# Weight sums of an encoder layer: accumulating transfers in place of VectorE additions

## The chip, the cores and the metric

The kernel runs on one core of a Trainium2 chip. The metric is the device time of one execution in microseconds. Before the change it is 1713.99 us, the median of three runs (1713.55 to 1715.02).

## The reference, cut to what matters

One layer of a bidirectional encoder, for two groups of 256 tokens with 1024 channels each, all in float32:

```
x = x + 0.5 * swiglu(rms_norm(x, g1), w_gate1, w_up1, w_down1)      # width 2816
u = rms_norm(x, gm);  proj = u @ w_in                               # one combined projection
o_na  = neighborhood_attention(q, k, v, rpb)                        # 16 heads of 64
o_ssd = two-way scan of conv(x, B, C), gated and group-normed
o_mem = memory_attention(q_mem, k_mem, v_mem)                       # 256 memory tokens
x = x + (sum_b sigmoid(gate_b) * (o_b @ w_br_b)) @ w_out
x = x + 0.5 * swiglu(rms_norm(x, g2), w_gate2, w_up2, w_down2)
```

Most of the work is products of 512 token rows with weight matrices.

## The kernel before, in words

**Products.** Every float32 matrix is split into a high part, rounded to a shorter format that TensorE takes, and a low part, the rest. A product is then three matmuls: high by high, low by high, high by low. For the weights the split is made on the fly: ScalarE casts the raw block `wr` to `wh` (line 349) and VectorE subtracts, `wl = wr - wh` (through the helper at line 248). The matmuls of a block product are at line 627 (`product`), those of plain products at lines 605 to 607 (`unit`).

**Seven products instead of eight.** The large projections (gate and up of both FFNs; query of the memory branch, values, and both halves of query and key of the neighbourhood branch) use a two-by-two block scheme with seven block products per column block. `seven` builds them: for each product p it adds an item to the list `ITEMS` with the blocks to load, the block to use, and `sums`, pairs of blocks (d, x) of which x is added into d before d is used. Products 5, 6, 7 and 4 have one sum each: B11 += B12, B11 += B22, B12 += B22, B11 += B21. So d is a raw block in SBUF of 128 x 1024 float32, often already used by an earlier product, and x is another one. A column block 512 wide is cut into two halves along the contraction (h = 0, 1), so it has 14 items and eight sums; the last block of an FFN is 256 wide and has seven items and four sums.

**Stages.** `make_plan` lists the items: the first FFN (column blocks 0 to 5; its block 0 is made without the scheme, so it has no sums), the memory keys and values, then a middle stage with four sets of seven products (`qm`, `v`, `qk` 0, `qk` 1, kind `sv`), then gates, branches, convolutions and scan, the output projection, and the second FFN (blocks 0 to 5). In an FFN, down-projection items of the block before stand between the pairs of products. In the sets nothing stands between them in the plan, but small tasks (attention and the like) are stepped in.

**Loading and summing.** Raw blocks live in a ring of nine slots (`RING`); `fetch` loads them ahead by SyncE's queue (line 302). A slot becomes free when the last use of its block is done, which is a split or a sum. `ahead` splits items up to two ahead of the product in hand; three pairs of `wh` and `wl` exist, so the cast of an item waits for the product three items before. `sums` makes the additions of the next items. If an item's flag `dma` is false, VectorE adds (line 248 again, output `wr`). If it is true, GpSimd's queue issues a transfer from SBUF to SBUF that adds to its destination (line 323), and `ahead` calls for it right after the split two items before:

```
if it.dma:
    self.G.dma_start(out=d, in_=v, accum_op=ALU.add)
else:
    self.tt(d, d, v, ALU.add)
```

Before the change the flag is true for three column blocks: set `qk` 1 and blocks 0 and 1 of the second FFN.

**Order.** The program is written in the order of `PLAN`. The framework keeps track of which instruction needs which, and orders each engine's queue when it builds the kernel; the trace shows sums on VectorE well ahead of where the program calls for them. Within a queue, the chip runs in order.

Of the kernel before, what the change touches and what calls it, by code (L numbers as in the profile page):

```python
# [39 lines left out]
ITEMS = []  # L40


def add_item(*args, **kw):
    ITEMS.append(Item(*args, **kw))
    return len(ITEMS) - 1
# [7 lines left out]
def seven(kind, p, key, block, nh):  # L53

    out = []
    for h in range(nh):  # L60
        n = lambda b: f"{kind}{key}.{h}.{b}"
        blk = lambda b: block(int(b[1]) - 1, int(b[2]) - 1, h)
        loads, src, sums = {1: (["B11"], "B11", []), 2: (["B21"], "B21", []), 5: (["B12"], "B11", [("B11", "B12")]),
                            6: (["B22"], "B11", [("B11", "B22")]), 3: ([], "B22", []), 7: ([], "B12", [("B12", "B22")]),
                            4: (["B21."], "B11", [("B11", "B21.")])}[p]
        _, _, nk, _, m = blk("B11")
        it = add_item(n(src), nk, m, [(n(b), blk(b)) for b in loads], [tuple(n(b) for b in t) for t in sums])
        ITEMS[it].dma = bool(sums) and (kind == "sv" and key == ("qk", 1) or kind == "gu" and key in (("ffn2", 0), ("ffn2", 1)))
        out.append((kind, (*key, p, h, nh), [it]))
    return out  # L70


def make_plan():
# [10 lines left out]
    def ffn(f):  # L84
# [5 lines left out]
        for ci, (c0, w) in enumerate(CBLOCKS + ((DFF, 0),)):  # L90
            n, down = w // 256, list(range(4)) if before else []

            def next_down():
                if down:
                    mp = down.pop(0)
                    s.append(("d", (f, ci - 1, mp), [plain(f + "_w_down", before[0], before[1], 256 * mp, 256)]))

            def part(p, ci=ci, c0=c0, w=w, n=n):
                s.extend(seven("gu", p, (f, ci), lambda i, j, h: (f + ("_w_up", "_w_gate")[j], 4 * i + 4 // n * h, 4 // n, c0, w), n))

            if f == "ffn1" and ci == 0:
                for j, mat in enumerate(("_w_up", "_w_gate")):
                    for c in range(4):
                        n = 1 if j == c == 0 else 2
                        s.append(("pl", (f, j, c), [plain(f + mat, 2 * c + i, n, c0, w) for i in range(0, 2, n)]))
            else:
                for p in PRODUCTS if w else ():
                    if p == 4 and ci == 0:
                        rest = part
                        continue  # L110
                    part(p)
                    if p == 1 and ci == 1 and f == "ffn2":
                        rest(4)
                    if p in ((5, 6, 3, 7) if n == 2 else (5, 3, 7, 4)):
                        next_down()
            for _ in range(4):
                next_down()
            before = (c0 // 128, w // 128)
# [15 lines left out]
    def sv(i, p):  # L134
        kind, c, *cols = sets[i]
        s.extend(seven("sv", p, (kind, c), lambda i, j, h: ("w_in", 4 * i + 2 * h, 2, cols[j], 512), 2))
# [1387 lines left out]
```

## Time and profile before

| what | value |
|---|---|
| median of three runs | 1713.99 us |
| profiled execution | 1712.59 us |
| span of its trace, first to last instruction | 1710.8 us |
| TensorE matmul (PE) | 1698.3 us busy, 99% |
| VectorE (DVE) | 1248.8 us, 73% |
| ScalarE (ACT) | 906.4 us, 53% |
| GpSimd (POOL) | 21.8 us, 1% |
| bytes moved by DMA | 241.69 MB, mean 141 GB/s |
| granted TensorE clock | 1.000 of full speed |

Busy shares are means over stages with different limits. A matmul is recorded as longer than the distance to the next one, since matmuls are pipelined; so the distance between starts tells the pace. Stretches are given in us from the span's start.

### The profile page before, as it was taken

How to read it: one execution, taken by the hardware profiler on the slowest of the kernel's cores; microseconds unless marked ns; L12 is line 12 of the kernel's file. 1: busy time of each engine (PE TensorE's matmuls, PEld its weight loads, DVE VectorE, ACT ScalarE, POOL GpSimd, SP SyncE). 2: the span in 40 equal slices, each digit the busy share in tenths (PEclk: the TensorE clock that was granted, in tenths of full speed). 3: DMA queues.
4: the chain of work that ended last, by engine and by line, in shares of the span. 5: the costliest groups of instructions: out<-in, count | busy, mean ns of one | idle time of the engine just before them, and what ended most of it. 6: DMA issues, size and time to landing. Idle time of an engine off the chain costs nothing.

```text
span 1710.8 us, 22582 instructions
## 1 busy us (share of the span) xinstructions
PE 1698.3 (99%) x8418; PEld 1396.5 (82%) x8418; DVE 1248.8 (73%) x2003; ACT 906.4 (53%) x1612; POOL 21.8 (1%) x30
## 2 busy tenths in 40 slices
PE   9999999999999999999999999999999999999998
PEld 7888888988888887788887887887788888888887
DVE  7776776877596675746978889888754775776775
ACT  7443443535455566654765677667532564443442
POOL 0000000000000000000000000000000010000000
PEclk9999999999999999999999999999999999999999
DMA  7234234443345675444364545346753487344331
GB/s 268 72 133 148 99 105 141 148 160 97 107 135 188 176 213 186 148 129 166 120 133 132 127 140 139 120 147 164 165 190 107 106 222 202 87 135 146 99 100 50
DMA packets 95070, 241.69 MB, mean 141 GB/s; under 512 B 13680, under 2 KB 24432, under 8 KB 94960
## 3 DMA queue, kind: packets, MB, share of 16 engines
q1 hardware_dynamic: 91504, 227.66, 42.6%
q0 software_dynamic: 3456, 12.58, 4.0%
q8 instruction: 66, 1.08, 0.3%
q14 instruction: 44, 0.36, 0.1%
HBM read 210.70 MB, written 16.92 MB: 133 GB/s over the span
## 4 chain that ended last, share of the span: by engine, by line
PE 54%; DVE 1%; DMA 1%; ACT 0%; issue 0%; SPq 0%; ACTq 0%
PE ac L627 12%; PE m L605 9%; PE m L607 9%; PE m L606 9%; PE m L1174 5%; PE d L606 2%; PE d L607 2%; PE d L605 2%; PE y L1395 2%; PE CB L1345 1%; DMA rw<-scr_n 1%; PE hT L756 1%; PE xT L1334 0%; PE sum L566 0%; DMA rw<-scr_r 0%; PE no L1091 0%
## 5 line engine op out<-in xcount | busy, mean ns | idle before, releaser
L349 ACT CAST wh<-wr 128x1024 fp32r<-128x1024 f32 (+1 forms) x381 | 395.9, 1039 | 594.2 <-PE ac L627 209.3
L248 DVE TENSOR_TENSOR wl<-wr,wh 128x1024 fp32r<-128x1024 f32 (+1 forms) x381 | 460.2, 1208 | 199.9 <-ACT wh L349 187.3
L627 PE MATMUL ac<-wh,sh 128*128 128x512 f32 (+1 forms) x744 | 281.2, 378 | 0.1
L627 PE MATMUL ac<-wh,sl 128*128 128x512 f32 (+1 forms) x744 | 278.1, 374 | 0.0
L627 PE MATMUL ac<-wl,sh 128*128 128x512 f32 (+1 forms) x744 | 278.1, 374 | 0.0
L605 PE MATMUL m<-uh,wh 128*128 128x512 f32 x576 | 229.5, 398 | 0.0
L606 PE MATMUL m<-ul,wh 128*128 128x512 f32 x576 | 224.8, 390 | 0.0
L607 PE MATMUL m<-uh,wl 128*128 128x512 f32 x576 | 224.8, 390 | 0.0
L627 PEld LDWEIGHTS ac<-wh,sh 128*128 128x128 f32 x744 | 140.2, 188 | 24.6 <-ACT wh L349 0.5
L627 PEld LDWEIGHTS ac<-wh,sl 128*128 128x128 f32 x744 | 140.1, 188 | 24.7
L627 PEld LDWEIGHTS ac<-wl,sh 128*128 128x128 f32 x744 | 140.3, 189 | 23.8
L606 PE MATMUL d<-hl,wh 128*128 128x512 f32 x352 | 137.3, 390 | 0.7 <-DVE hl L248 0.7
L605 PE MATMUL d<-hh,wh 128*128 128x512 f32 x352 | 137.4, 390 | 0.5 <-ACT hh L270 0.5
L607 PE MATMUL d<-hh,wl 128*128 128x512 f32 x352 | 137.0, 389 | 0.0
L605 PEld LDWEIGHTS m<-uh,wh 128*128 128x128 f32 x576 | 108.2, 188 | 27.8 <-ACT ct L263 4.2
L607 PEld LDWEIGHTS m<-uh,wl 128*128 128x128 f32 x576 | 108.1, 188 | 23.1 <-issue 0.4
L606 PEld LDWEIGHTS m<-ul,wh 128*128 128x128 f32 x576 | 108.3, 188 | 21.4 <-issue 0.2
L259 DVE SCALAR_TENSOR_TENSOR x<-d,x 128x512 f32<-128x512 f32 x96 | 66.1, 690 | 77.3 <-PE d L607 76.8
L248 DVE TENSOR_TENSOR wr<-wr,wr 128x1024 f32<-128x1024 f32 x88 | 107.4, 1221 | 9.6 <-DMA wr<-in_w 8.4
L263 ACT ACTIVATE e<-rw,lots 128x256 f32<-128x256 f32 (+1 forms) x256 | 97.4, 445 | 2.3 <-DMA rw<-scr_r 2.3
L259 DVE SCALAR_TENSOR_TENSOR cv<-m,params,cv 128x508 f32<-128x508 f32 (+1 forms) x128 | 95.0, 742 | 1.3
L606 PEld LDWEIGHTS d<-hl,wh 128*128 128x128 f32 x352 | 66.1, 188 | 14.8 <-DVE hl L248 1.4
(247 smaller groups left out, 2658.6 us busy)
## 6 DMA issues: line engine op xcount, KB each, us to landing
wr<-in_w SPq DMA_DIRECT2D x315, 512.0 KB
rw<-scr_r SPq DMA_DIRECT2D x64, 256.0 KB
wr<-wr POOLq DMA_DIRECT2D x24, 512.0 KB, 5.8
nv<-scr_v SPq DMA_DIRECT2D x64, 64.0 KB
scr_o<-cv SPq DMA_DIRECT2D x16, 256.0 KB
or<-scr_o SPq DMA_DIRECT2D x16, 256.0 KB
wr<-in_w SPq DMA_DIRECT2D x11, 256.0 KB
x<-in_xT SPq DMA_DIRECT2D x8, 256.0 KB
```

What stands on the lines that cost most here:

```text
L248: self.V.tensor_tensor(out=out, in0=a, in1=b, op=op)
L259: self.V.scalar_tensor_tensor(out=out, in0=a, scalar=s, in1=b, op0=op0, op1=op1)
L263: self.S.activation(out=out, in_=x, func=f, **kw)
L349: self.S.copy(hi[:, :n], t[:, :n])
L605: self.T.matmul(ps[:m], wh[:, kk, :], xh, start=i == 0, stop=False)
L606: self.T.matmul(ps[:m], wh[:, kk, :], xl, start=False, stop=False)
L607: self.T.matmul(ps[:m], wl[:, kk, :], xh, start=False, stop=i == n - 1)
L627: go = lambda l, r, **f: self.T.matmul(ps, l, r, skip_group_check=True, **f)
L756: self.T.transpose(ps[:, (2 * r + t) * 128:(2 * r + t + 1) * 128], o["sg", r, t][:, c * 128:(c + 1) * 128], self.ident)
L1174: go = lambda l, r, **f: self.T.matmul(ps, l, r, skip_group_check=True, **f)
L1345: T.matmul(ps[:, st * 256:(st + 1) * 256], bm[:, b * 256 + st * 128:b * 256 + (st + 1) * 128], cm[:, b * 256:(b + 1) * 256], start=True, s ...
L1395: T.matmul(yb[64 * hp:64 * hp + 64, b * 256:(b + 1) * 256], xt[i][:, (2 * b + st) * 128 + 64 * hp:(2 * b + st) * 128 + 64 * hp + 64], w[hp ...
```

## The change

The condition for the flag `dma` is replaced. All column blocks with sums now have them made by transfers on GpSimd's queue, except block 1 of the first FFN.

```diff
@@ seven @@
         it = add_item(n(src), nk, m, [(n(b), blk(b)) for b in loads], [tuple(n(b) for b in t) for t in sums])
-        ITEMS[it].dma = bool(sums) and (kind == "sv" and key == ("qk", 1) or kind == "gu" and key in (("ffn2", 0), ("ffn2", 1)))
+        ITEMS[it].dma = bool(sums) and key != ("ffn1", 1)
```

Of 112 sums, 24 were transfers and 88 additions on VectorE; now 104 are transfers and 8 are additions. The order of the items, the loads and the splits in the program stays as it is, but for the place where `ahead` calls `sums`.

## Rows read from the trace of the kernel before

**Rows 1.** Page, part 1: busy us (share of the span) x instructions.
```profile
PE 1698.3 (99%) x8418; PEld 1396.5 (82%) x8418; DVE 1248.8 (73%) x2003; ACT 906.4 (53%) x1612; POOL 21.8 (1%) x30
```

**Rows 2.** Waits of TensorE, longest first: us in total, times, longest us.
```profile
PE y L1395 <- DVE e L248: 2.4, 2, 1.5
```

**Rows 3.** Chain of waits, second FFN's blocks 1 and 2: start us, us, what.
```profile
1426.66 5.44 PE ac L627 x24
...
1459.30 6.81 PE ac L627 x30
...
1488.48 5.44 PE ac L627 x24
...
1521.12 6.80 PE ac L627 x30
```

**Rows 4.** Page, part 5: groups of instructions: busy us, mean ns of one, idle before, releasers.
```profile
L248 DVE TENSOR_TENSOR wr<-wr,wr 128x1024 f32<-128x1024 f32 x88 | 107.4, 1221 | 9.6 <-DMA wr<-in_w 8.4
```

**Rows 5.** Groups on TensorE, 445 to 600 us, then 1462 to 1524.
```profile
L627 PE MATMUL ac<-wh,sh 128*128 128x512 f32 x96 | 38.5, 403 | 0.1
...
L627 PE MATMUL ac<-wh,uh 128*128 128x512 f32 x76 | 30.7, 404 | 0.0
...
L605 PE MATMUL d<-hh,wh 128*128 128x512 f32 x32 | 12.4, 389 | 0.0
```

**Rows 6.** Line 323 and its queue: ns min/median/max; share of 16 engines.
```profile
q0 software_dynamic: 3456, 12.58, 4.0%
...
L323 POOL DMA_DIRECT2D wr<-wr x24: 859/869/1118, 583.6 to 1435.8; - x24
...
DMA to landing us min/median/max: 4.5/5.8/8.3
```

**Rows 7.** Timeline, second FFN's block 0: start us, us, instruction, idle before and releaser.
```profile
1371.89 1.22 DVE L248 TENSOR_TENSOR wl<-wr,wh 128x1024 fp32r<-128x1024 f32 x1
...
1373.51 0.87 POOL L323 DMA_DIRECT2D wr<-wr  x1 [3.91 <-DVE y L290]
...
1378.69 1.05 ACT L349 CAST wh<-wr 128x1024 fp32r<-128x1024 f32 x1 [3.85 <-PE ac L627]
...
1381.19 0.39 PE L627 MATMUL ac<-wh,sh 128*128 128x512 f32 x1
...
1381.22 1.05 ACT L349 CAST wh<-wr 128x1024 fp32r<-128x1024 f32 x1 [1.48 <-DMA wr<-wr]
...
1383.91 0.39 PE L627 MATMUL ac<-wh,sh 128*128 128x512 f32 x1
```

**Rows 8.** Stretches: length, busy us of PE, PEld, DVE, ACT, POOL; clock; DMA share; GB/s.
```profile
445.00:504.00 59.00, 58.94 (x265) 47.83 (x265) 52.18 (x70) 32.01 (x51) 0.00 (x0) 1.00 0.38 125
504.00:558.00 54.00, 53.96 (x254) 44.64 (x253) 40.41 (x68) 30.37 (x65) 0.00 (x0) 1.00 0.47 159
...
1352.00:1400.00 48.00, 48.00 (x217) 39.78 (x216) 38.25 (x65) 31.29 (x43) 7.81 (x9) 1.00 0.75 172
1400.00:1462.00 62.00, 62.00 (x283) 51.54 (x282) 37.00 (x42) 26.59 (x32) 6.09 (x7) 1.00 0.75 211
1462.00:1524.00 62.00, 62.00 (x283) 51.35 (x282) 45.21 (x49) 26.80 (x33) 0.00 (x0) 1.00 0.38 119
```

**Rows 9.** Timeline, first FFN's 256-wide block.
```profile
296.01 1.22 DVE L248 TENSOR_TENSOR wl<-wr,wh 128x1024 fp32r<-128x1024 f32 x1 [0.21 <-ACT wh L349]
...
316.38 0.28 PE L627 MATMUL ac<-wh,sh 128*128 128x256 f32 x1
```

**Rows 10.** Timeline, first set of the middle stage.
```profile
461.38 1.23 DVE L248 TENSOR_TENSOR wl<-wr,wh 128x1024 fp32r<-128x1024 f32 x1 [1.50 <-ACT wh L349]
...
471.54 0.39 PE L627 MATMUL ac<-wh,sh 128*128 128x512 f32 x1
```

**Rows 11.** Waits of SyncE's queue: us in total, times, longest us.
```profile
SPq L302 <- DVE wl L248: 998.4, 233, 15.9
...
SPq L302 <- DMA wr<-wr: 33.4, 6, 11.7
```

## The prediction

> **What bounds the kernel now.** I read the busy shares first, then who made TensorE wait and the chain of waits, then the rows of the additions that move, then stretches that already have the new form. The busy shares put PE at 1698.3 of 1710.8 us [rows 1]; all its idle time is 12.5 us. VectorE is busy for 73%. The list of what TensorE waited for, longest first, begins with a VectorE result of the scan, not of the block products: 2.4 us in all, in two instances [rows 2]; all the rest is shorter. The chain of waits then follows TensorE through the product blocks [rows 3]. So TensorE is the bound from its first matmul to its last, and something is worth time only if it removes or adds a TensorE stall. "Busy" can hide a short stall, so beside busy shares I use mean durations and start times of matmuls.
>
> **What is removed.** The row of the additions has 88 instructions, 107.4 us, 1.22 us each [rows 4]. 24 others already go by POOL. The new condition is false for one block of the first FFN only, whose two halves have four sums each: 8 stay, 80 go. That is 80 x 1.221 = 97.7 us of VectorE work, or 1248.8 - 97.7 = 1151 us, 67% of the span. VectorE is off the path, so this is worth at most the stalls that VectorE causes. In the weight products of the middle stage the first of the three matmuls on a weight slice lasts 403 ns (96 of them) and 404 ns (76), where a matmul of the same shape in an FFN block lasts 389 ns [rows 5]: 96 x 14 + 76 x 15 ns = 2.5 us of stall, from whatever cause. That is the ceiling of the gain there; in the large blocks, below, it is 0. I take 0, because the nearest rows with the change in them show no gain.
>
> **What is added.** 80 transfers on POOL's queue. One issue takes 0.87 us of POOL, and from issue to landing 4.5 / 5.8 / 8.3 us pass (least, median, most of 24) [rows 6]. POOL has nothing else after its first microsecond, so queueing there touches only the sums. A sum now ends about 0.4 us (POOL's start behind the releasing split: 1371.89 + 1.22 = 1373.11 to 1373.51 [rows 7]) plus L = 5.8 us after its release instead of 1.2 us. Behind it stand the ACT cast (1.05 us) and the VectorE subtraction (1.22 us) of the same block [rows 7], 2.3 us together, and then the product. ACT is in order: while a cast waits for a transfer, the copies behind it that empty PSUM wait too. SP also is in order: a load that needs the slot of a summed-in block waits for the transfer, not for VectorE.
>
> All of this assumes that the builder, which orders every queue at build time, keeps the order of today's around the sums; where it moves a cast earlier, that cast waits longer.
>
> What hides it, by kind of stretch:
>
> *Six 512-wide FFN blocks, 48 of the 80 sums.* The trace holds this change already. Of two neighbouring blocks of the second FFN, 1400 to 1462 us has its sums on POOL and 1462 to 1524 us has them on VectorE: VectorE busy falls from 45.21 to 37.00 us, DMA share rises from 0.38 to 0.75, and TensorE is 62.00 of 62.00 in both [rows 8]. In the chain of waits the same two pieces start 1459.30 - 1426.66 = 32.64 us apart in the first and 1521.12 - 1488.48 = 32.64 us apart in the second [rows 3]. Cost 0.0 us per block, gain 0.0 us. The other blocks have the same plan, so 6 x 0 = 0. The transfers hide here because a 5.4 us down-projection stands between the pairs of products; without it the cover is that of the next kind.
>
> *Two 256-wide blocks (8 sums).* No block of this shape has transfers yet, so I add up. In the first, the split that releases sum 5 ends at 296.01 + 1.22 = 297.2. With L: sum landed at 297.6 + L, split done at 299.9 + L. This split releases the sum of product 6: landed at 300.3 + 2L, split at 302.6 + 2L. Product 6 starts at 316.38 [rows 9]. Its slack is 13.8 - 2L: zero at L = 6.9 us, +2.2 at the median, -2.8 at 8.3. The block in the second FFN has the same plan. Cost between 0 and 2 x 2.8 = 5.7 us; I take 0, by the median.
>
> *Three sets of the middle stage (24 sums).* The densest is the first, where products follow each other every 2.7 us with nothing between. The split that releases the sum of product 6 ends at 461.38 + 1.23 = 462.6, and its product starts at 471.54 [rows 10]; 462.6 + 0.4 + L + 2.3 = 465.3 + L, so it decides at L = 6.2. Nearest row: the first block of the second FFN is as dense, and its sums are transfers. There the split ends at 1373.1, POOL issues at 1373.51, ACT casts at 1378.69, and the product starts at 1381.19; the next cast waits for its transfer until 1381.22 and its product follows at 1383.91, 2.72 us after, exactly on the pace [rows 7]. 8.1 us from split to product was enough there, and the first set has 8.9. In the other two sets attention work stands between the products and widens the distance. Cost between 0 and 2.1 us (L = 8.3); I take 0.
>
> **DMA engines.** The 24 transfers made 4.0% of 16 engines' span [rows 6]: 0.040 x 1710.8 / 24 = 2.85 us of all sixteen each. In 504 to 558 us a third of the middle stage's sums, eight, would add 22.8 us to a share of 0.47 of 54 us [rows 8]: 0.89. The stretch measured with transfers stood at 0.75 and lost nothing [rows 8]. Below 1 I cost this at 0. SP already spends 998 us waiting for slots behind VectorE's splits and 33 us behind such transfers [rows 11]: its loads run ahead, and five more microseconds on the two slots per block that a sum sets free come out of that lead.
>
> **The sum.** -0 (VectorE) + 0 (large blocks) + 0 (256-wide) + 0 (middle stage) = 0 on the profiled execution: 1712.59 us with a span of 1710.8. The median of the three runs, 1713.99, stands 1.40 us above that execution, so I forecast 1714.0 for the median.
>
> **Rivals.**
>
> *Late landing (slower).* The transfers land later than the median once 104 of them share the engines with the loads. Place: the first set of the middle stage and the two 256-wide blocks. It decides from L = 6.2 there and 6.9 here; at L = 7.85 it costs 1.6 + 2 x 1.9 = 5.4 us: 1719.4. At the worst measured L, 8.3, 2.1 + 5.7 = 7.8: 1721.8. For it: the median is only 0.4 us below the first limit, the worst row is above both, and one cast already waited 1.48 us for a transfer [rows 7]. Against: those transfers landed 5.2 us after issue, in a stretch with a DMA share twice that of a plain FFN block, and both are short places.
> VectorE could also hold POOL back. The slowest of 24 issues took 1.118 us against a median of 0.869 [rows 6], beside a busy VectorE. Were POOL held for one whole VectorE instruction, 1.22 us, L would be 7.0 and the sum 0.8 + 2 x 0.2 = 1.2 us: 1715.2; the 0.25 us between slowest and median issue speak against that.
> The Trainium skill (SBUF — State Buffer, "SBUF: two separate sides") states that GpSimd and VectorE share a port pair that one of them locks for a whole instruction, and that a VectorE instruction in a two-port mode so keeps GpSimd from writing a transfer's descriptors. By that rule the 1715.2 would come about; the trace disagrees as far as its 24 issues go.
>
> *Engines run full (slower).* In the middle stage loads arrive late because the share goes to 1. For it: 0.89 in one window. Against: 0.75 without loss. Its price: one load that comes a full landing late, 5.8 us: 1719.8.
>
> *VectorE's relief counts (faster).* The 2.5 us of the middle stage go, and about as much in the attention work between, which waits for VectorE too: -5 us at most, -3.5 us as its middle, 1710.5. For it: VectorE is busy 52.18 of 59 us around the first set [rows 8]. Against: the 2.5 us above are all the stall that these products show, and not all of it is VectorE's.
>
> That the sums would not move is no case: the flag alone picks POOL.
>
> **How the numbers follow.** Some 0.2%, 3.4 us, is what a measurement of this kernel can tell from none. Forecast (within 1710.6 to 1717.4): 0.69. Late landing 0.16 and full engines 0.06: slower 0.22. Faster 0.09. Range: down to 1709.5, most of the faster case; up to 1720.5, which takes in late landing up to L = 8.1: of the faster case 0.03, of the two slower ones 0.10 are left out.
>
> **What would show it.** Right: VectorE's row of sums with 8 instructions, POOL with 104, VectorE busy near 1151 us, PE still 1698 us, pieces in the FFN blocks still 32.64 us apart, and waits of ACT casts for such transfers of a few us in number but none of TensorE behind them. Wrong: gaps in TensorE at product 6 of the first set or of the 256-wide blocks, a median landing over 6.2 us, loads named before casts, or a span shorter by more than 3 us, which would mean that VectorE set the pace somewhere that I read as free.

## The result, and the profile after

The kernel became slower: 1723.08 us (median of four, 1721.49 to 1724.48) against 1713.77 us (four, 1712.85 to 1715.02), ratio 1.0051 with a 95% interval of 1.0039 to 1.0064. That is 9.3 us, above the range of the prediction (1709.5 to 1720.5). The profiled execution took 1722.93 us, with a span of 1721.2 us.

Most of the rows that were forecast are there; VectorE is busy for 1160.8 us, not 1151. The page's part 1 (against [rows 1]) and the queue of the transfers in its part 3 (packets, MB, share of 16 engines; against [rows 6]):

```profile
PE 1701.9 (99%) x8418; PEld 1399.5 (81%) x8418; DVE 1160.8 (67%) x1923; ACT 903.4 (52%) x1612; POOL 91.5 (5%) x110
...
q0 software_dynamic: 14976, 54.53, 17.2%
```

The group of sums left on VectorE (busy us, mean ns; against [rows 4]):

```profile
L248 DVE TENSOR_TENSOR wr<-wr,wr 128x1024 f32<-128x1024 f32 x8 | 9.8, 1223 | 0.4 <-DMA wr<-in_w 0.2
```

Line 323, the transfers (ns of one issue and us from issue to landing, each min/median/max; against [rows 6]):

```profile
L323 POOL DMA_DIRECT2D wr<-wr x104: 859/869/1221, 112.8 to 1673.0; - x104
...
DMA to landing us min/median/max: 4.5/6.4/9.9
```

TensorE's idle time is not on the page's top line (99% again); it is in its list of waits (us in total, times, longest). Against [rows 2] four kinds are new: a cast and a subtraction of the split in the block products, a transpose `hT` in the FFN, and one (`tr`) in the attention work.

```profile
PE ac L627 <- ACT wh L349: 3.4, 1, 3.4
PE y L1395 <- DVE e L248: 2.2, 1, 2.2
PE hT L756 <- DVE hl L248: 1.6, 2, 0.8
...
PE tr L942 <- ACT qkT L263: 1.1, 1, 1.1
PE ac L627 <- DVE wl L248: 1.0, 2, 0.8
```

**Where the time went.** Both traces run the same products in the plan's order, so I compared the start of every product's first matmul and took the growth of the delay from place to place. The wide FFN blocks are 0.91 us shorter in all; the two 256-wide blocks cost 1.60, the first middle set (`qm`) 6.01, set `v` 1.60, set `qk` 0 0.01. That is 8.3 us. Another 0.64 us stands before the first products and 1.32 us at one wait of the scan; the experiments below speak against this last one being the change's.

**The first set.** The timeline, POOL first (the pair at 464.87 is merged; its second stands behind it by itself), then VectorE, ScalarE and TensorE (start us, us, instruction, idle before and releaser):

```profile
449.21 0.86 POOL L323 DMA_DIRECT2D wr<-wr  x1 [134.58 <-DVE wl L248]
455.54 1.76 POOL L323 DMA_DIRECT2D wr<-wr  x2 [5.46 <-DMA scr_m<-vm]
464.87 1.76 POOL L323 DMA_DIRECT2D wr<-wr  x2 [7.57 <-DMA wr<-wr]
465.41 1.22 POOL L323 DMA_DIRECT2D wr<-wr  x1
467.30 0.89 POOL L323 DMA_DIRECT2D wr<-wr  x1 [0.66 <-DVE wl L248]
...
462.40 1.23 DVE L248 TENSOR_TENSOR wl<-wr,wh 128x1024 fp32r<-128x1024 f32 x1 [1.50 <-ACT wh L349]
...
472.21 1.04 ACT L349 CAST wh<-wr 128x1024 fp32r<-128x1024 f32 x1 [6.58 <-DMA wr<-wr]
...
469.55 0.39 PE L627 MATMUL ac<-wh,sl 128*128 128x512 f32 x1
473.31 0.50 PE L627 MATMUL ac<-wh,sh 128*128 128x512 f32 x1 [3.38 <-ACT wh L349]
474.57 0.51 PE L627 MATMUL ac<-wl,sh 128*128 128x512 f32 x1 [0.76 <-DVE wl L248]
...
476.30 0.63 PE L627 MATMUL ac<-wl,sh 128*128 128x512 f32 x1
476.73 0.63 PE L627 MATMUL ac<-wh,sl 128*128 128x512 f32 x1
```

The queue's order, which the framework wrote, is product 5 (first half), 7 (first), 5 (second), 7 (second), 6, 6. Product 7's sum overwrites a block that product 5's transfer reads, so it waits for that landing, and all behind it wait too. Product 6's first sum was free when the split before it ended, at 462.40 + 1.23 = 463.63 us (VectorE's `wl`); it is the second of the pair, so it was issued only at 465.41, 1.78 us later (the expectations of e5 and e9 below give 465.75, from the merged row). Its cast could start at 472.21, 6.80 us after the issue. TensorE waited 3.38 us for the cast and 0.76 for the subtraction. Then its clock was granted at half, 1.2 GHz: from 476.30 the matmuls start 0.43 us apart instead of 0.23. The granted clock by stretch (start and end; length; busy us of PE, PEld, DVE, ACT, POOL; clock; DMA share; GB/s):

```profile
468.00:474.00 6.00, 2.43 (x10) 1.44 (x8) 0.79 (x2) 1.77 (x2) 0.18 (x1) 1.00 1.07 203
474.00:478.50 4.50, 3.93 (x10) 2.78 (x11) 4.20 (x7) 1.46 (x3) 0.87 (x1) 0.62 0.54 102
```

The half clock lasted 3.4 us, in which half the work was done: 1.7 us. With 3.38 + 0.76 that makes 5.8 of the 6.0 us. The Trainium skill (TensorE: Matmul & The Clock Gate, "Wait — 56ns, not 53.3ns?") gives 426.7 ns from start to start for 512 columns on a cold array; the trace agrees with its 0.43 us.

**The 256-wide blocks.** In the first of them, ScalarE and then TensorE:

```profile
302.69 1.05 ACT L349 CAST wh<-wr 128x1024 fp32r<-128x1024 f32 x1 [3.58 <-DMA wr<-wr]
303.64 0.37 ACT L728 COPY s<-ac 128x256 f32<-128x256 f32 x1
303.90 1.08 ACT L270 CAST hh<-hT 128x512 fp32r<-128x512 f32 x2
...
305.65 0.44 PE L756 MATMUL hT<-consts,u 128*128 128x128 f32 x2 [0.79 <-DVE hl L248]
```

The cast for product 5 stands at the head of ScalarE's queue and waits 3.58 us for its transfer. The instructions that empty PSUM stand behind it, among them the cast `hh` of a transpose; VectorE's subtraction `hl` needs `hh`, and TensorE's next transposes wait 0.79 us for `hl`.

**Set `v`.** POOL, ScalarE and TensorE:

```profile
510.90 0.86 POOL L323 DMA_DIRECT2D wr<-wr  x1 [2.62 <-DVE wl L248]
...
519.83 1.04 ACT L349 CAST wh<-wr 128x1024 fp32r<-128x1024 f32 x1 [7.87 <-DMA wr<-wr]
...
521.51 0.66 PE L942 MATMUL tr<-consts,qr 128*128 128x128 f32 x4 [1.13 <-ACT qkT L263]
```

Here product 6's first transfer was issued 0.40 us after the split that frees it (VectorE's `wl` ended at 510.50), but its cast could start only 8.93 us after the issue. The activation `qkT` of the attention work stands behind that cast on ScalarE, and TensorE's transposes waited 1.13 us for it.

**Issue and landing.** The waits of POOL for such landings (us in total, times, longest), before and after:

```profile
POOL wr L323 <- DMA wr<-wr: 17.2, 4, 6.1
...
POOL wr L323 <- DMA wr<-wr: 89.4, 23, 9.2
```

The landing itself depends on the queue too. Counted over the trace's records, 41 of the 104 transfers were issued after the one before had landed, and took 5.3 us at the median; 63 were issued while it was still under way, and took 7.1 us. None landed ahead of one issued earlier. In the trace before it was 12 of each kind, 5.0 and 7.1 us.

**The wide blocks.** Chain of waits, second FFN's blocks 1 and 2, against [rows 3]:

```profile
1436.72 5.44 PE ac L627 x24
...
1469.36 6.81 PE ac L627 x30
...
1498.37 5.44 PE ac L627 x24
...
1531.01 6.80 PE ac L627 x30
```

The pieces are 32.64 us apart in both blocks, as before. From block to block it is 1498.37 - 1436.72 = 61.65 us where it was 1488.48 - 1426.66 = 61.82 [rows 3].

### The profile page after: what moved, and what is told of

Same layout as the page of the kernel before. It is cut to its first block, busy times and chain, and to the rows that moved or that the text cites. A ratio compares the mean times of both kernels' runs of the same rounds, so it can differ in the third digit from the quotient of the medians.

```text
span 1721.2 us, 22744 instructions
## 1 busy us (share of the span) xinstructions
PE 1701.9 (99%) x8418; PEld 1399.5 (81%) x8418; DVE 1160.8 (67%) x1923; ACT 903.4 (52%) x1612; POOL 91.5 (5%) x110
## 3 DMA queue, kind: packets, MB, share of 16 engines
q0 software_dynamic: 14976, 54.53, 17.2%
## 4 chain that ended last, share of the span: by engine, by line
PE 52%; DMA 2%; issue 1%; DVE 1%; ACT 0%; SPq 0%; POOLq 0%; ACTq 0%
PE ac L627 11%; PE m L605 9%; PE m L607 9%; PE m L606 9%; PE m L1174 5%; PE d L606 2%; PE d L607 2%; PE d L605 2%; PE y L1395 2%; PE CB L1345 1%; DMA wr<-wr 1%; DMA rw<-scr_n 1%; PE hT L756 0%; PE xT L1334 0%; PE sum L566 0%
## 5 line engine op out<-in xcount | busy, mean ns | idle before, releaser
L323 POOL DMA_DIRECT2D wr<-wr x104 | 90.7, 885 | 1581.8 <-DVE wl L248 1265.9
```

## The experiments

The table has, for each kernel, the delay gained against the kernel before (us) at four places by the starts of TensorE's products in the two profiled executions, their sum, and the measured difference (ratio with 95% interval, each against the runs of the kernel before on the same chip). "Scan" is the delay at the scan's wait, which is not in the sum.

| kernel | wide | 256-wide | `qm` | `v` | sum | ratio (interval) | scan |
|---|---|---|---|---|---|---|---|
| the change | -0.91 | 1.60 | 6.01 | 1.60 | 8.3 | 1.0051 (1.0039-1.0064) | 1.32 |
| e1 | -0.91 | 1.60 | 0.01 | 0.81 | 1.5 | 1.0008 (0.9999-1.0016) | 0.43 |
| e2 | 0.09 | 0.01 | 6.75 | 1.15 | 8.0 | 1.0038 (1.0025-1.0050) | 3.71 |
| e3 | -0.85 | 0.02 | 0.02 | -0.03 | -0.8 | 0.9994 (0.9985-1.0003) | 3.67 |
| e4 | 0.21 | 1.65 | 0.04 | 1.17 | 3.1 | 1.0011 (1.0002-1.0020) | 1.06 |
| e5 | 0.76 | 0.02 | 6.45 | 1.01 | 8.2 | 1.0048 (1.0033-1.0063) | 2.40 |
| e6 | 0.37 | 0.02 | 1.31 | 0.03 | 1.7 | 1.0012 (1.0002-1.0021) | 1.46 |
| e7 | 0.14 | 0.01 | 0.25 | 3.26 | 3.7 | 1.0018 (1.0009-1.0028) | 1.88 |
| e8 | 0.07 | 0.02 | -0.43 | 9.64 | 9.3 | 1.0066 (1.0051-1.0081) | 3.35 |
| e9 | -0.96 | 1.55 | 1.21 | 1.93 | 3.7 | 1.0029 (1.0019-1.0038) | 3.18 |
| e10 | -0.90 | 1.60 | -0.43 | 9.79 | 10.1 | 1.0053 (1.0040-1.0067) | 0.93 |
| e11 | -0.91 | 1.59 | -0.04 | 1.49 | 2.1 | 1.0014 (1.0005-1.0023) | 1.17 |
| e12 | -0.92 | -0.42 | 0.01 | -0.03 | -1.4 | 0.9992 (0.9983-1.0001) | 1.39 |
| e13 | -0.96 | -0.42 | -0.43 | -0.05 | -1.9 | 0.9997 (0.9988-1.0006) | 4.15 |

0.001 of ratio is 1.7 us. The four places account for the differences within the intervals, in all fourteen; what kernels that leave the wide blocks alone show there, 0.07 to 0.76, I take for scatter between executions. The scan's wait is longer in every trace than in that of the kernel before, but by 0.4 to 4.2 us without regard to the change: it is 3.67 in e3, which has no other transfer near it and whose runs are not slower. So I take it for the execution's: the traced execution of the kernel before (1712.59 us) is among the shortest of its runs, which lie between 1712.6 and 1718.4 us. With one trace of each kernel this isn't shown.

### By place: e1 to e4

```diff
 e1, from the changed kernel
-ITEMS[it].dma = bool(sums) and key != ("ffn1", 1)
+ITEMS[it].dma = bool(sums) and key not in (("ffn1", 1), ("qm", 0))
 from the kernel before, to the blocks that had transfers (set qk 1, second FFN's 0 and 1):
+e2: ("qm", 0)
+e3: blocks 2 to 4 of both FFNs
+e4: block 5 of both FFNs, ("v", 0), ("qk", 0)
```

e1. 

> The changed kernel with the eight sums of the first middle set (qm) put back on VectorE; 72 of the 80 stay transfers. Theory (late sum): of the 10.4 us that the changed kernel's profiled run lost along TensorE, 6.1 us were lost at product 6 of this set, where the cast at 472.21 us waited 6.58 us for a transfer and TensorE 3.38 us for the cast, with the clock at half for 3.4 us after it. Then this kernel takes about 1723.1 - 6.1 = 1717.0 us (1715.5 to 1718.5), and the clock does not fall near 475 us. Rival (engines or POOL's queue loaded everywhere, loss in proportion to transfers): 8 of 80 sums carry 8/80 x 9.3 = 0.9 us, so 1722.2. Rival (the gap only moves: VectorE's row of sums or the next set takes it over): above 1720.

e2. 

> The kernel before with only the eight sums of the first middle set made into transfers. Theory (late sum): the whole stall is there, 1713.8 + 6.1 = 1719.9 us (1718.4 to 1721.4), with TensorE waiting some 3.4 us for a cast and the clock at half behind it. Rival (proportion to transfers): 1713.8 + 0.9 = 1714.7. Rival (it takes the other transfers beside it to make these land late): under 1716, with landing near 4.5 to 5.8 us and no drop of the clock.

e3. 

> The kernel before with only the 48 sums of the six 512-wide FFN blocks made into transfers. Theory: these blocks gained 0.17 us each in the changed kernel's trace, so 1713.8 - 1.0 = 1712.8 us (1711.8 to 1714.0), VectorE 58.6 us less busy. Rival (proportion to transfers): 48/80 x 9.3 = 5.6 us, 1719.4. The step of the prediction (0 each): 1713.8.

e4. 

> The kernel before with only the sums of the two 256-wide FFN blocks and of the sets v and qk0 made into transfers (24 of the 80). Theory by the traces: 0.8 us for each 256-wide block, 1.6 us for v, 0 for qk0: 1713.8 + 3.2 = 1717.0 us; if the longer wait and the half clock near 1222 us (1.3 us, in the gates) belong to the change, they have no transfer near them and come in any kernel or none. Rival (proportion to transfers): 24/80 x 9.3 = 2.8 us, 1716.6, but spread over all three kinds. The step of the prediction (0): 1713.8.

Measured: 1716.39, 1722.17, 1714.67 and 1716.94 us against 1715.38 (the expectations start from 1713.8, so the differences count). By place all four follow the theory; e1 and e4 stand only 1.0 and 1.6 us over the kernel before where 3.2 were expected, as their traces show 0.81 and 1.17 us in `v` instead of 1.60, and e1's 0.43 at the scan instead of 1.32. In e2 the half clock lasted 6.8 us instead of 3.4, and `qm` cost 6.75. The rival of a loss in proportion to the transfers is out: eight transfers in `qm` cost 6.5 us (e2), 48 in the wide blocks nothing that the runs show (e3). e2 also shows that the other 72 transfers are not needed for the stall.

### Inside the first set, from the kernel before: e5 to e8

```diff
+kind == "sv" and key == ("qk", 1) or ... or key == ("qm", 0) and p in P
 e5: P = (5, 6, 4); e6: (6,); e7: (5, 7, 4); e8: (5, 6, 7, 4), and in make_plan
-    a("dt", 0, "w_in", COL_DT, m=64)
     ...
             sv(i, p)
+            if (i, p) == (0, 5):
+                a("dt", 0, "w_in", COL_DT, m=64)
```

e5. 

> The kernel before with the first middle set's sums of products 5, 6 and 4 as transfers and those of product 7 on VectorE; all eight as transfers cost +6.8 us (1722.17 against 1715.38). Theory, queue: POOL runs its transfers in order, and the two of product 7 stand ahead of the ones that product 6 needs, waiting for the landing of product 5's; the split that frees product 6's sum ended at 463.63 us in the changed kernel and its transfer was issued at 465.75. Without them it goes out about 1.9 us sooner, so TensorE's wait of 3.0 us falls to 1.1 and the clock drop behind it (half for 6.8 us, about 3.4 us) shrinks or goes: +1.4 to +4.8 us over before. Rival, landing alone: the order on POOL does not matter, the landing is late by itself: +6 to +7 us as with all eight. Rival, product 7 was the whole cause: +0 to +0.7 us.

e6. 

> The kernel before with only the two sums of product 6 of the first middle set as transfers (5, 7 and 4 on VectorE). Nothing else stands in POOL's queue then, so this is the landing by itself. The split that frees the sum ends at about 462.6 us as in the kernel before; with 0.3 us to the issue, 4.5 to 5.8 us to land and 1.05 us of cast the product can start at 468.5 to 469.8, where TensorE wants it at 468.75. Theory (both queue and landing): a wait of 0 to 1.1 us and no or one short clock drop: +0 to +2.8 us. Rival, queue alone: +0 to +0.3. Rival, landing alone is the cause: +6 us or more.

e7. 

> The kernel before with the first middle set's sums of products 5, 7 and 4 as transfers, and only product 6's two on VectorE. Theory: product 6 is the only one that is late; +0 to +0.8 us over before, no wait of TensorE for a cast of this set above 1 us, no drop of the clock near 473 us. Rival: product 5's sums land late as well, or ACT's copies are held up behind casts that wait for them, and that costs as much: +3 us or more.

e8. 

> The kernel before with all eight sums of the first middle set as transfers, and the 16 matmuls of the dt projection (3.6 us), which run just ahead of the set, moved between products 5 and 6. Theory: product 6 is wanted 3.6 us later against the releasing split, and with the wait of 3.0 us the clock drop goes too: +0 to +1 us over before. Rival: with dt gone from ahead of the set product 5's own sum comes late and the stall moves there, +3 to +7 us. Rival, the transfers cost TensorE in another way than by the distance: +6.8 us, as without the move.

Measured against 1714.52: 1723.46, 1716.39, 1718.18, 1726.12. Only e6 came as the theory said: its transfer was issued at 463.31 and cast at 468.10, 4.8 us later; TensorE waited 0.76 us, and the set lost 1.3 us. POOL, ScalarE and TensorE in e6:

```profile
463.31 1.00 POOL L323 DMA_DIRECT2D wr<-wr  x1 [462.01 <-DMA wr<-in_w]
...
468.10 1.05 ACT L349 CAST wh<-wr 128x1024 fp32r<-128x1024 f32 x1 [3.66 <-DMA wr<-wr]
...
470.47 0.50 PE L627 MATMUL ac<-wl,sh 128*128 128x512 f32 x1 [0.76 <-DVE wl L248]
```

The other three expectations missed by more than their intervals, and by the traces each for the same reason: a waiting instruction came to the head of VectorE's queue. In e5 it was product 7's addition (timeline of VectorE):

```profile
463.44 1.23 DVE L248 TENSOR_TENSOR wr<-wr,wr 128x1024 f32<-128x1024 f32 x1 [5.10 <-DMA wr<-wr]
464.58 3.49 DVE L248 TENSOR_TENSOR wl<-wr,wh 128x1024 fp32r<-128x1024 f32 x3
```

VectorE waited 5.10 us for product 5's landing, as POOL had, and three subtractions then ran together; so product 6's transfer was issued only at 467.23 us. e5 did not test the queue; it moved it. In e8 the set itself lost nothing (-0.43 us), but in set `v`, whose sums are on VectorE there, two additions waited for their loads ahead of the subtractions, and TensorE's clock was at half twice. VectorE's timeline in e8, and then its stretches (columns as above):

```profile
489.16 1.23 DVE L249 TENSOR_TENSOR wr<-wr,wr 128x1024 f32<-128x1024 f32 x1 [2.60 <-DMA wr<-in_w]
```

A second addition of set `v`, at 491.90, waits 1.31 us for its load; the two stretches at half clock follow.

```profile
494.00:498.00 4.00, 3.69 (x10) 2.92 (x11) 4.00 (x6) 0.00 (x0) 0.00 (x0) 0.57 0.00 1
...
511.00:515.00 4.00, 4.00 (x12) 3.15 (x11) 3.93 (x15) 1.22 (x2) 0.00 (x0) 0.57 0.16 61
```

e7's total is what its rival gave, but the rival's place, `qm`, lost only 0.25 us: e7 lost 3.3 us in `v`, with the same kind of row (a wait of 2.91 us for a load).

### In the changed kernel, where no set's sums are on VectorE: e9 to e11, and e12

```diff
 e9, sums (cut): each transfer of qm is put behind the one before it
+                if it.dma and "qm" in it.src:
+                    with self.tc.issue_after(self.last) if self.last else nullcontext():
+                        self.last = self.G.dma_start(out=d, in_=v, accum_op=ALU.add).ins
 e10: dt moved as in e8
 e11
+... and (key, p) != (("qm", 0), 6)
 e12
+... and key not in (("ffn1", 1), ("qm", 0), ("v", 0)) and not (kind == "gu" and key[1] == 5 and p == 5)
```

e9. 

> The changed kernel, with POOL made to issue the eight transfers of the first middle set in the order of the products (5, 6, 7, 4); today product 7's first stands second in POOL's queue and its second fourth, ahead of product 6's, each waiting for a landing of product 5's. Nothing moves to another engine, so no other queue gets a new head that waits. Theory, queue and landing: product 6's transfer goes out right behind the split that frees it, some 2 us sooner (465.75 to about 463.8 us); what is left is the landing by itself, which cost 1.9 us with product 6's sums alone. So the 10 us over before fall by 2 to 4.5 us: 1718.5 to 1721 us. Rival, landing alone: the order makes no difference, 1723. Rival, the loads: product 7's later transfers free slots later, loads for the next set come late, and set v loses what this one gains: 1722 to 1724, with the wait moved behind 488 us.

e10. 

> The changed kernel with the 16 matmuls of the dt projection moved between products 5 and 6 of the first middle set. In the kernel before, with only that set as transfers, this move took the stall of TensorE at product 6 away, but VectorE's own sums of set v then stood at the head of its queue, waiting for loads that came late, and 10 us were lost there. In the changed kernel set v's sums are not on VectorE. Theory: both go, 1723.1 - 6.1 = 1717.0 us (1716 to 1718.5), no half clock near 475 us. Rival: the late loads alone cost the 10 us, whoever adds: 1722 or more. Rival, distance is not what matters: 1723.

e11. 

> The changed kernel with only the two sums of product 6 of the first middle set back on VectorE; 78 of the 80 stay transfers. Theory: these two are the ones that TensorE waits for; in the kernel before with the same set their return left 0.8 us in the set, so 1723.1 - 5.3 = 1717.8 us (1716.5 to 1719). Rival: product 6 only shows a delay of the whole set, which the other six sums keep up: 1721 or more. Rival: VectorE's queue gets a head that waits and set v loses it again, as in the kernel before with that set: 1720 to 1722.

e12. 

> The changed kernel with the sets qm and v back on VectorE, and of the two 256-wide FFN blocks the sums of product 5 alone: 62 of the 80 stay transfers. Theory: the 256-wide blocks lose 0.8 us each because ScalarE's cast for product 5 stands ahead of the casts that empty PSUM and waits 3.6 us for its transfer; without that wait they lose nothing, set qk 0 loses nothing, and the six wide blocks gain 0.17 us each: 1.0 us under the kernel before. Rival: the 256-wide blocks are late at product 6 or 7 as well and still lose 0.8 us each: 0.6 us over it. By the medians of a few runs the two are just apart; the starts of products 2 and 5 in these blocks tell it in the trace.

Measured against 1714.88: 1719.74, 1723.93, 1717.16, 1713.70. e9 is the clean test of the queue: the same 80 transfers, those of `qm` in another order. Its timeline, POOL, ScalarE and TensorE (its line numbers are 1 to 6 higher):

```profile
463.62 0.88 POOL L327 DMA_DIRECT2D wr<-wr  x1 [8.51 <-DVE wl L249]
...
468.27 1.05 ACT L355 CAST wh<-wr 128x1024 fp32r<-128x1024 f32 x1 [3.59 <-DMA wr<-wr]
...
470.63 0.50 PE L633 MATMUL ac<-wl,sh 128*128 128x512 f32 x1 [0.77 <-DVE wl L249]
471.77 0.50 PE L633 MATMUL ac<-wh,sh 128*128 128x512 f32 x1 [0.17 <-DVE qr L260]
```

Product 6's transfer is issued 0.40 us behind its split (461.99 + 1.23 = 463.22) instead of 1.78, with nothing under way ahead of it, and its cast starts 4.65 us after the issue instead of 6.80. TensorE waits 0.77 us for the subtraction and 0.17 us for VectorE's `qr`, and no half clock follows. The set's loss falls from 6.01 to 1.21 us, which is e6's 1.31, the landing by itself. e11 confirms from the other side: without product 6's two sums the set loses nothing (-0.04).

e10 missed: dt's 3.6 us took the loss out of `qm`, and `v` then lost 9.79 us with its sums on POOL. The framework had ordered POOL's queue 5, 7, 5, 7, 6, 6 in `v` too (in the change it is 5, 5, 7, 7, 6, 6 there). The timeline of POOL (the pair at 508.50, then its second by itself), VectorE, ScalarE and TensorE in e10:

```profile
508.50 1.75 POOL L324 DMA_DIRECT2D wr<-wr  x2 [9.52 <-DMA wr<-wr]
509.04 1.21 POOL L324 DMA_DIRECT2D wr<-wr  x1
...
501.14 1.22 DVE L249 TENSOR_TENSOR wl<-wr,wh 128x1024 fp32r<-128x1024 f32 x1
...
517.62 1.04 ACT L350 CAST wh<-wr 128x1024 fp32r<-128x1024 f32 x1 [8.37 <-DMA wr<-wr]
...
519.30 1.97 PE L1279 MATMUL loc<-dt,consts 128*128 128x64 f32 x8 [5.90 <-ACT qkT L264]
```

The split that frees product 6's first sum ended at 501.14 + 1.22 = 502.36 us; its transfer is the second of the pair and was issued at 509.04, 6.7 us later, behind product 7's. The cast waited for it until 517.62, TensorE waited 5.90 us for the activation `qkT` behind that cast, and the clock was at half in that stretch (columns as above):

```profile
515.50:526.00 10.50, 6.70 (x24) 6.02 (x25) 4.61 (x5) 6.34 (x9) 0.87 (x1) 0.51 0.63 132
```

e10's time is also what its rival of the late loads gave; e13 below decides between the two.

e12 shows the 256-wide blocks free of loss with product 5's sums on VectorE (-0.21 us each instead of +0.80; TensorE's waits for `hT` are gone). At 0.9992 its interval just reaches 1, so it is not shown faster than the kernel before.

### Order and distance together: e13

```diff
 e13: dt moved as in e8; e9's order for all sv items; and
+... and not (kind == "gu" and key[1] == 5 and p == 5)
```

> The changed kernel with three things: POOL issues the transfers of all four middle sets in the order of the products; dt's 16 matmuls stand between products 5 and 6 of the first set; product 5's sums of the two 256-wide blocks are back on VectorE. 78 of the 80 stay transfers. Theory (queue order and distance are the whole cause): 0 in the first set, about 1 us in set v (its landings by themselves), 0 in the 256-wide blocks, -1.0 us in the wide blocks: as the kernel before, within 0 to +1.5 us. Rival: the transfers make the loads of set v late whatever the order, and the 9 us that set v lost when dt alone was moved come back: +8 to +10 us. Rival: the order only moves the wait from product 6 to product 7, behind whose sums the loads of the next set stand: +3 to +6 us.

Measured: 1714.92 us against 1715.03. 78 of the 80 sums are transfers and cost nothing that the runs or the four places show. e13 differs from e10 in the order of the sets' transfers and in two sums of other blocks, and set `v` loses -0.05 us instead of 9.79; so it was the order. (The move of dt without transfers was not run; the 0.43 us that `qm` gains with it may be its own.) One row answers the rival of the full engines as well, a stretch of the first set (columns as above): TensorE is busy throughout at a DMA share of 1.04.

```profile
465.00:475.00 10.00, 10.00 (x45) 7.78 (x45) 3.67 (x3) 5.59 (x7) 0.97 (x2) 1.00 1.04 216
```

## Why the prediction was wrong, step by step

*VectorE's relief is worth 0*: right. Its row of sums fell from 107.4 to 9.8 us, as computed. VectorE as a whole fell by 88.0 us and not by 97.7. Summed over the records, its other instructions are 5.3 us longer in all, each a little; the remaining 4.4 us come from records that overlap their neighbours, which busy time counts once. e3, e12 and e13 show no gain beyond 1 to 2 us, which the intervals don't separate from none.

*Six wide blocks, 0*: right within 0.15 us each (measured -0.91 in all, not separate from none in e3's runs).

*First set, "decides at L = 6.2"*: this step failed, in three terms.

First, the start of product 6 was misread. I took the row at 471.54 [rows 10] for it. The kernel before:

```profile
465.90 0.48 PE L627 MATMUL ac<-wh,sh 128*128 128x512 f32 x1
...
468.75 0.39 PE L627 MATMUL ac<-wh,sh 128*128 128x512 f32 x1
468.98 0.39 PE L627 MATMUL ac<-wl,sh 128*128 128x512 f32 x1
```

TensorE's order of instructions runs product 5 for the first half of the token rows (12 matmuls from 465.90), then begins product 6 at 468.75, before product 5's other half is done (ScalarE's copies of the two halves start at 468.95 and 474.78). So the second matmul at 468.98 wants the subtraction's result: 465.3 + L has to be under 468.98, L under 3.7 us. The least landing was 4.5 [rows 6], which gives a stall of 0.8 us at least; e6 and e9 measured 0.76 and 0.77. The right row was in the trace.

Second, POOL's queue was given no cost ("queueing there touches only the sums"). But sums block each other: POOL waited 89.4 us for landings of such transfers, and 17.2 us already before the change. And L was taken from all 24 transfers, where those issued behind one still under way had a median of 7.1 us, above the limit of 6.2 as well. The queue made 4.8 of the 6.0 us (e9 against the change: 6.01 - 1.21), 1.7 of them by the half clock that the longer stall brought, and the landing itself 1.2.

Third, the clock had no term at all.

*"The builder keeps the order around the sums"*: false. It was written as the assumption that carried the rest. POOL's order is not the products' order; the order changed again in nearly every experiment.

*Two 256-wide blocks, "decides at L = 6.9" at product 6*: right form, wrong product. They lost 0.8 us each at product 5's cast, through ScalarE's queue, which the text named ("the copies behind it that empty PSUM wait too") and never priced. (In its sum, 2 x 2.8 is 5.6 and not 5.7, which decides nothing.)

*Sets `v` and `qk` 0, 0*: `qk` 0 was free; `v` lost 1.60 us, and -0.05 with the queue in order (e13). The attention work that was to widen the distance there stands itself behind the late cast on ScalarE.

*DMA engines, 0 below a share of 1*: right, and even at 1.04 (e13). So the rival of full engines is out.

*The rival of late landing* named the two places and 1721.8 us at worst. The median landing did rise, to 6.4 us, but that is not what it cost: in e13 the landings of all 102 transfers have a median of 6.6 us, and nothing is lost. It was given 0.16, and the limit that this rested on stood 2.5 us too high.

*VectorE holding POOL back* (the rule of the Trainium skill weighed there): one issue takes 869 ns at the median, as before. The six issues of 1.03 to 1.22 us in the change that stand right behind another are long with VectorE busy or idle; of the 98 others 46 ran beside VectorE for over 0.7 us, and 44 of these took under 0.90 us. So the trace bears out no such hold.

## What to carry to other kernels

Work moved from an engine to a DMA queue is ordered by that queue: list the queue's entries in their order, and for each ask what it waits for and what stands behind it; one entry that waits for another's landing can cost more than the landings themselves (4.8 against 1.2 us in the first set here). Take the time at which a consumer is wanted from the consumer's own queue and from its first instruction, since a scheduler may begin a product in the middle of another. A distance of a few microseconds is worth nothing in the sum until the least landing, the cast and the subtraction fit in it.

## What was not expected of the hardware

For the same sum of 512 KB the cast could start 4.65 us after the issue in e9 and 6.80 us after it in the change, where the transfer was issued 0.54 us behind another. The Trainium skill (DMA: Bandwidth & Descriptors, "Anatomy of one DMA — SWDGE (gpsimd) path") has a fit that gives 2.0 + 524288/436000 = 3.2 us for this size, an estimate by which the landing alone would have been in time (under 3.7); the 104 transfers took 4.5 us at least, so the measurement decides. A stall of 3.38 and 0.76 us was followed by half clock for 3.4 us, one of 0.77 and 0.17 us (e9) by none. The length of a wait alone doesn't tell it: 1.48 us in e7's set `v` (ended at 497.86) was followed by half clock from 498.45, 2.71 and 0.87 us at the scan in e11 by none. The delay at the scan's wait varied by 4 us between kernels that don't differ there.
